# Gathering the narrow-tile products of sparse attention in TensorE's instruction order

## The chip, the cores and the metric

One core of a Trainium2 chip runs the whole program. The metric is the device time of one execution in microseconds, the median of several runs; lower is better.

## The reference, cut to what matters

One inference step of a decoder layer with two mixers that share one input projection, for a prompt of 256 tokens and 8 sample sequences of 8 tokens with 2,048 cached tokens each (320 token columns in all):

```python
u = rmsnorm(x) @ w_in                       # 2048 x 23664, split among all mixers
o_a = gated_delta(conv(qkv_a), z_a, ...)    # 32 heads of 128, recurrent state
o_cmp, idx = cmp_select(q, pos, kc, vc, ...)          # pooled blocks of keys; top-16 blocks per query
o_sel = select_sample(q, pos, idx, cache_k_sel, cache_v_sel, page_table, ...)
o_win = window_sample(q, pos, cache_k_win, cache_v_win, ...)
o_b = (g[0] * o_cmp + g[1] * o_sel + g[2] * o_win) * silu(z_b)
y = x + (sigmoid(m_a) * (o_a @ w_branch_a) + sigmoid(m_b) * (o_b @ w_branch_b)) @ w_out
```

For the sample sequences the sparse attention (o_cmp, o_sel, o_win) has few query rows: 4 heads of a group x 8 tokens are 32 rows, for each of 4 key groups. Everything is float32.

## The kernel before, in words

The dense projections are one long stream, `p_mm` (with `p_load`, `p_hi`, `p_lo`): weights come in tiles `wraw` of 1 MB through a ring of three (`NRC`), ScalarE rounds each piece of four 128-row blocks to float32r (`whi`), VectorE forms the rest (`wlo`), and TensorE adds three products `acc` of 128x320 per 128 rows. Rings of four pieces (`NHI`) let the splitting run ahead of the products by 48 products. This stream has the lowest priority; it fills TensorE where nothing else is ready.

Beside it run generators for the other work. In the sparse attention stage these are `prompt` (the prompt's attention, full tiles), `compressed` (pooling of the cached pages, `pp`, then scores `sc`, sums `ip`, output `oc`), `window` (512 cached keys per sequence) and, from about a third of the program on, two workers `sample`, four sequences each, that read all pages of the selected cache. `scores` transposes a page (`nt`), copies it (`kT`, by VectorE and ScalarE in turn) and multiplies it with the queries (`ns`); `weighted` transposes the weights (`nt` from `xs`), copies them (`pT`) and multiplies them with the pages of values (`op`). The products `pp`, `sc`, `ns`, `op`, `oc` have 32 output rows each; four of them, one per key group or page, lie side by side in column tiles of TensorE (128x32, or 64x32 for the 64 new keys). `mp` uses 32 rows (32x128). All other products and transpositions use the whole 128x128 array. Pages come through SyncE's queue into slots (`Feed`), 10 per worker (`SW`).

The order of all engines' instructions is fixed when the program is built. A class `Clock` holds an estimated time per engine and the estimated end of every tile's last write and read; a class `Run` holds the generators. Each generator yields what its next step needs: an engine's name with tiles, such as `("pe", e.sum)`, or a condition. `Run._start` (L354) turns this into the earliest start by the estimate: the engine's own time or the moment at which the inputs are ready, whichever is later. `Run.go` takes the step with the earliest start, the smaller rank where two are equal, and lets it emit its instructions. `Clock.narrow` says whether the last product used a part of the array; `Timed` adds 170 ns to the estimate where this changes (the line `if self.clock.narrow != part`).

Then comes the gated DeltaNet stage (`g_init`, `conv_stream`, `g2_stream`, `g3_stream` and more; its first TensorE products go to `bank`, its constants are `c`, `pk_gdn` and `pk_gini`), and at the end the projections of the two branches and `w_out`. After the sample stage `obS` is stored to `d_ob` through SyncE's queue, which holds its instructions in order.

Of the kernel before, what the change touches and what calls it, by code (L numbers as in the profile page):

```python
# [37 lines left out]
NRC = 3  # L38
NHI = 4
NPL = 4  # L40
CR = -1
OR = -4
NWP = 4
# [20 lines left out]
class Pack:  # L64
    def __init__(self, rows=P):
        self.at, self.parts, self.n, self.rows = {}, [], 0, rows
# [267 lines left out]
class Run:  # L334
# [2 lines left out]

    def __init__(self, clock):  # L340
        self.c, self.s = clock, []

    def add(self, gen, rank=0, at=None):
        x = [gen, None, (self.c.t["pe"], "sp") if at is None else at, rank]
# [12 lines left out]
    def _start(self, x):  # L357
        if callable(x[1]):
            while callable(x[1]):
                if not x[1]():  # L360
                    return None
                self._step(x)
                if x not in self.s:
                    return None
        y = x[1]
        e = y[0] if isinstance(y, tuple) else y
        if e == "exp":
            if self.c.lock:
                return None
            e = "act"  # L370
        if not isinstance(y, tuple):
            return max(self.c.t[e], self.c.after(x[2], e))
        return max([self.c.t[e]] + [self.c.after(a, e) if isinstance(a, tuple) else a.free(e) if isinstance(a, Next) else
                                    self.c.ready(e, a) for a in y[1:]])

    def go(self, until=lambda: False):
        while self.s and not until():
# [58 lines left out]
def step(ctx: ExitStack, tc: tile.TileContext, I, O):  # L436
    nc = tc.nc
    ctx.enter_context(tc.manual_schedule())
    clock = Clock()
# [39 lines left out]
    run = Run(clock)  # L479
# [688 lines left out]
    def pooled(b, kv):  # L1168
        pp = cps.tile([P, 512], F32, tag="a", name="pp")
        for i in range(0, 4, 2):  # L1170
            pg = []
            for _ in range(8):
                pg.append((yield from cfeed.get()))
            yield ("pe", *pg)
            for k in range(8):
                j = k % 4
                T.matmul(pp[32 * j:32 * j + 32], Pk[:, kv, i + k // 4], pg[k], start=i + k // 4 == 0, stop=i + k // 4 == 3)
            if i == 0:
                for j in range(3):
                    T.matmul(pp[32 * j:32 * j + 32], Pk[:, kv, 4], pg[j + 1], start=False, stop=False)  # L1180
            cfeed.release(8)
        yield "dve"
        pl = cp.tile([P, 512], F32, tag="c0", name="pl", bufs=1)
        V.tensor_tensor(pl.rearrange("p (g d) -> p g d", g=4), pp.rearrange("p (g d) -> p g d", g=4),
                        bc(cb[:, kv], [[0, 4], [1, P]]), op=OP.add)
        yield ("pe", clock.last, Next(cps, "a"))
        tp = cps.tile([P, 512], F32, tag="a", name="tp")
        for g in range(4):
            T.transpose(tp[:, g * P:g * P + P], pl[:, g * P:g * P + P], ident)
        yield "act"  # L1190
        pt = cp.tile([P, 512], F32, tag="c1", name="pt", bufs=1)
        S.activation(pt, tp, AF.Copy)
        yield "pe"
        return pt

    def compressed():
        for b in range(B):
            pt = yield from pooled(b, 0)
            yield lambda: done["q"] == 16
            yield ("pe", clock.last, Next(cps, "a"))  # L1200
            kp = cps.tile([P, 512], F32, tag="a", name="kp")
            T.matmul(kp, proj[:, 0], pt, start=True, stop=True)
            rs = yield from rstd(cp, cps, "a", kp, 512, (0, 512), ("c0", "c2", "c3"))
            kc = cp.tile([P, 512], F32, tag="c0", name="kc", bufs=1)
            V.scalar_tensor_tensor(kc, kp, gains[:, 1:2], rs, op0=OP.mult, op1=OP.mult)
            yield ("pe", clock.last, Next(cps, "a"))
            sc = cps.tile([P, 512], F32, tag="a", name="sc")
            for g in range(4):
                T.matmul(sc[32 * g:32 * g + 32, :127], qT(b, g), kc[:, g * P:g * P + 127], start=True, stop=True)
            yield "dve"  # L1210
            s1 = cp.tile([P, 127], F32, tag="s1", name="s1")
            V.scalar_tensor_tensor(s1, sc[:, :127], SCALE, cmpB[:, :127], op0=OP.mult, op1=OP.add)
            mx = cp.tile([P, 3], F32, tag="mxc", name="mxc")
            V.tensor_reduce(mx[:, 0:1], s1, axis=AX.X, op=OP.max)
            V.tensor_scalar(mx[:, 0:1], mx[:, 0:1], -1.0, None, op0=OP.mult)
            yield "act"
            S.activation(s1, s1, AF.Exp, bias=mx[:, 0:1], accum_out=mx[:, 1:2])
            yield "dve"
            V.reciprocal(mx[:, 2:3], mx[:, 1:2])
            V.tensor_scalar(s1, s1, mx[:, 2:3], None, op0=OP.mult)  # L1220
            yield ("pe", clock.last, Next(cps, "a"))
            ip = cps.tile([P, 512], F32, tag="a", name="ip")
            q = 32 * (b % 4)
            T.matmul(ip[q:q + 32, :127], N["G"], s1, start=True, stop=True)
            T.transpose(ip[:127, P:2 * P], s1, ident)
            yield "dve"
            V.tensor_copy(imp[q:q + 32, b // 4, :127], ip[q:q + 32, :127])
            sT = cp.tile([P, P], F32, tag="sT", name="sT")
            V.tensor_copy(sT[:127], ip[:127, P:2 * P])
            if b % 4 == 3:  # L1230
                yield from select(b // 4)
                done["sel"] = b // 4 + 1
            pt = yield from pooled(b, 1)
            vp = cps.tile([P, 512], F32, tag="a", name="vp")
            for g in range(4):
                T.matmul(vp[:, g * P:g * P + P], pt[:, g * P:g * P + P], proj[:, 1], start=True, stop=True)
            yield "dve"
            vc = cp.tile([P, 512], F32, tag="c0", name="vc", bufs=1)
            V.tensor_copy(vc, vp)
            yield ("pe", clock.last, Next(cps, "a"))  # L1240
            oc = cps.tile([P, 512], F32, tag="a", name="oc")
            for g in range(4):
                T.matmul(oc[32 * g:32 * g + 32, :P], sT[:127, 32 * g:32 * g + 32], vc[:127, g * P:g * P + P], start=True, stop=True)
            yield "dve"
            add_o(oc, gS[:, 0, b:b + 1], b)
            done["cmp"] = b + 1
# [55 lines left out]

    def new_scores(e, bs, kS, dst):

        yield ("pe", e.sum)
        ns = e.s("ns")
        for i, b in enumerate(bs):
            for g in range(4):
                T.matmul(ns[32 * g:32 * g + 32, 64 * i:64 * i + 64], qT(b, g), kS[:, g], start=True, stop=True)
        for i, b in enumerate(bs):  # L1310
            yield ("dve", ns)
            V.scalar_tensor_tensor(dst[:, i], ns[:, 64 * i:64 * i + 64], SCALE, newB[:, 56 - 8 * b:120 - 8 * b], op0=OP.mult, op1=OP.add)

    def scores(e, b, npg, finish):

        for quad in range(0, npg, 4):
            ks, ns = [], None
            for p in range(4):
                pg = yield from e.feed.get()
                yield ("pe", pg, e.next)  # L1320
                nt = e.t("nt")
                for g in range(4):
                    T.transpose(nt[:, g * P:g * P + P], pg[:, g * P:g * P + P], ident)
                e.feed.release()
                ks.append(e.x("kT", e.nk))
                if p % 2:
                    yield ("dve", nt)
                    V.tensor_copy(ks[-1], nt)
                else:
                    yield ("act", nt)  # L1330
                    S.activation(ks[-1], nt, AF.Copy)
                if len(ks) < e.nk:
                    continue
                yield ("pe", *ks, *([] if ns else [e.sum]))
                ns = ns or e.s("ns")
                for k, kT in enumerate(ks, p + 1 - e.nk):
                    for g in range(4):
                        T.matmul(ns[32 * g:32 * g + 32, k * P:k * P + P], qT(b, g), kT[:, g * P:g * P + P], start=True, stop=True)
                ks = []
            yield ("dve", ns)  # L1340
            finish(quad, ns)

    def weighted(e, b, npg, x, vS, op):

        pend = []
        for quad in [npg] + list(range(0, npg, 4)) + [None]:
# [8 lines left out]
            if quad not in (0, npg):  # L1355
# [2 lines left out]
                    for k in range(n0):  # L1358
                        got.append(((yield from e.feed.get()) if q0 < npg else vS, pT, k, m0))
                last = quad is None  # L1360
                yield ("pe", *[y[0] for y in got], *[y[3] for y in pend])
                for i, (pg, pT, k, m0) in enumerate(got):
                    for g in range(4):
                        T.matmul(op[32 * g:32 * g + 32], pT[:m0, k * P + 32 * g:k * P + 32 * g + 32], pg[:m0, g * P:g * P + P],
# [56 lines left out]
    def sample(smp, sps, n, bs):  # L1421
# [4 lines left out]
        for i, b in enumerate(bs):  # L1426
            yield lambda: done["sel"] > b // 4
            q = 32 * (b % 4)
            yield ("pe", selm, Next(sps, "s"))
            mp = sps.tile([P, 512], F32, tag="s", name="mp")  # L1430
            T.matmul(mp[:, :32], N["E"][q:q + 32], selm[q:q + 32, b // 4], start=True, stop=True)
            yield "dve"
# [782 lines left out]
        slab(I["w_branch_b"], DM, ((256 * f, 256),), KT, Later("b", 0), Later("b", 1), lambda f: True, take_b(2 * f), None, lambda k: fin["ob"] > k)  # L2215

    pj["gdn"] = True
    run.add(g_init())
    run.add(load_z_stream(), -1)
    run.add(conv_stream(), 2)  # L2220
# [126 lines left out]
```

## Time and profile before

| what | value |
|---|---|
| median of 3 runs | 2573.67 us (2572.28 to 2574.88) |
| the profiled execution | 2573.57 us, span 2571.4 us |
| TensorE busy | 2518.8 us, 98%, 22,220 records |
| TensorE's weight load | 2325.0 us, 90% |
| VectorE, ScalarE, GpSimd busy | 64%, 54%, 16% |
| granted TensorE clock, mean | 0.994 |
| DMA, mean | 214 GB/s, 549.12 MB |

TensorE is the engine to look at; a share of 98% says that it waits little, not that all its time is spent well. A record's length is its latency: products overlap, so costs are read from the distance of starts. All products are recorded under one line, L330, that of the helper that emits them, so groups are told apart by their tiles.

### The profile page before, as it was taken

What the parts mean: (1) busy time and instruction counts of PE and PEld (TensorE: products, weight loads), DVE (VectorE), ACT (ScalarE), POOL (GpSimd) and SP (SyncE); (2) the same over time, 40 slices, a digit from 0 to 9 for tenths busy, and PEclk for the clock granted to TensorE, in tenths of its full rate; (3) what the DMA queues carried; (4) which work ended last, traced back from release to release, by engine and by line L of the source; (5) the groups of instructions that cost most, each with busy time, mean ns of one, the idle gap of its engine ahead of it and who ended that gap; (6) DMA issues with size and microseconds to landing.
All of it is one profiled execution on the core that took longest, in us unless ns stands there. A gap on an engine that the chain in (4) does not pass through costs nothing.

```text
span 2571.4 us, 59460 instructions
## 1 busy us (share of the span) xinstructions
PE 2518.8 (98%) x22220; PEld 2325.0 (90%) x22220; DVE 1645.7 (64%) x4090; ACT 1400.4 (54%) x3290; POOL 413.2 (16%) x991
## 2 busy tenths in 40 slices
PE   7999999999999999999999999999999989999999
PEld 5898788888899888889999999998999979999999
DVE  5554455555756555544788788788797875555443
ACT  5453443444444333335777868777787755544443
POOL 2000001000000000000133234243334232000000
PEclk9999999999999999999999999999999999999999
DMA  6757777888875889985554655555456546765564
GB/s 197 236 165 250 240 250 280 280 295 303 277 254 180 317 273 316 320 260 171 169 177 138 194 161 172 162 171 176 135 173 192 193 147 211 229 195 180 185 194 126
DMA packets 553795, 549.12 MB, mean 214 GB/s; under 512 B 32994, under 2 KB 457107, under 8 KB 553123
## 3 DMA queue, kind: packets, MB, share of 16 engines
q1 hardware_dynamic: 538660, 496.30, 60.4%
q0 software_dynamic: 14848, 49.04, 5.3%
q8 instruction: 175, 2.87, 0.4%
q14 instruction: 112, 0.92, 0.1%
HBM read 472.93 MB, written 72.29 MB: 212 GB/s over the span
## 4 chain that ended last, share of the span: by engine, by line
PE 83%; issue 6%; DVE 5%; DMA 2%; POOL 2%; ACT 1%; SPq 0%; DVEq 0%; POOLq 0%; ACTq 0%
PE acc L330 60%; PE ps L330 6%; PE nt L330 3%; PE pp L330 3%; PE op L330 2%; PE ns L330 1%; POOL vx L330 1%; PE bank L330 1%; PE tp L330 1%; DVE wlo L330 1%; PE p L330 1%; PE ms L330 1%; PE pu L330 1%; PE sp L330 1%; DMA spg<-cache_k_sel 1%
## 5 line engine op out<-in xcount | busy, mean ns | idle before, releaser
L330 PE MATMUL acc<-hhi,whi 128*128 128x320 f32 (+1 forms) x3472 | 1154.8, 333 | 0.7 <-ACT hhi L330 0.7
L330 ACT ACTIVATE whi<-wraw 128x512 fp32r<-128x512 f32 (+1 forms) x996 | 625.8, 630 | 847.4 <-PE acc L330 797.5
L330 PE MATMUL acc<-hhi,wlo 128*128 128x320 f32 (+1 forms) x3472 | 1077.6, 310 | 0.7 <-DVE wlo L330 0.7
L330 PE MATMUL acc<-hlo,whi 128*128 128x320 f32 (+1 forms) x3472 | 1076.4, 310 | 0.1
L330 DVE TENSOR_TENSOR wlo<-wraw,whi 128x512 fp32r<-128x512 f32 x992 | 681.7, 691 | 529.3 <-ACT whi L330 501.0
L330 PEld LDWEIGHTS acc<-hhi,whi 128*128 128x128 f32 (+1 forms) x3472 | 657.8, 189 | 38.4 <-issue 29.6
L330 PEld LDWEIGHTS acc<-hlo,whi 128*128 128x128 f32 (+1 forms) x3472 | 658.2, 190 | 6.9 <-issue 2.6
L330 PEld LDWEIGHTS acc<-hhi,wlo 128*128 128x128 f32 (+1 forms) x3472 | 655.4, 189 | 0.9 <-DVE wlo L330 0.9
L330 PE MATMUL acc<-oah,whi 128*128 128x320 f32 x512 | 158.2, 309 | 0.0
L330 PE MATMUL acc<-oal,whi 128*128 128x320 f32 x512 | 158.2, 309 | 0.0
L330 PE MATMUL acc<-oah,wlo 128*128 128x320 f32 x512 | 158.2, 309 | 0.0
L330 POOL CAST vx<-v 32x128 fp32r<-32x128 f32 x256 | 97.8, 382 | 115.2 <-DVE v L330 84.2
L330 DVE SCALAR_TENSOR_TENSOR cv<-xp,cw,cv 128x344 f32<-128x344 f32 x192 | 111.0, 578 | 5.6 <-ACT cv L330 4.0
L298 POOL DMA_DIRECT2D d_mz<-raw x48 | 26.2, 545 | 466.8 <-ACT raw L330 418.8
L330 PEld LDWEIGHTS acc<-oah,whi 128*128 128x128 f32 x512 | 96.1, 188 | 0.0
L330 PEld LDWEIGHTS acc<-oal,whi 128*128 128x128 f32 x512 | 96.1, 188 | 0.0
L330 PEld LDWEIGHTS acc<-oah,wlo 128*128 128x128 f32 x512 | 96.1, 188 | 0.0
L330 DVE SCALAR_TENSOR_TENSOR sS<-sS,ends,pu 128x128 f32<-128x128 f32 x256 | 83.2, 339 | 14.5 <-PE pu L330 14.0
L330 DVE COPY kT<-nt 128x512 f32<-128x512 f32 x80 | 55.0, 690 | 57.7 <-PE nt L330 56.5
L330 PE MATMUL pp<-cpg,Pk 128*32 128x512 f32 x608 | 78.6, 598 | 0.0
L330 ACT ACTIVATE kT<-nt 128x512 f32<-128x512 f32 x80 | 47.1, 594 | 57.3 <-PE nt L330 57.2
L330 PE MATMUL nt<-pk_const,spg 128*128 128x128 f32 x512 | 76.1, 276 | 1.6 <-DMA spg<-cache_k_sel 1.6
(422 smaller groups left out, 3412.9 us busy)
## 6 DMA issues: line engine op xcount, KB each, us to landing
wraw<-w_in SPq DMA_DIRECT2D x120, 1024.0 KB
wraw<-w_in SPq DMA_DIRECT2D x129, 512.0 KB
cpg<-cache_k_cmp SPq DMA_DIRECT2D x128, 256.0 KB
cpg<-cache_v_cmp SPq DMA_DIRECT2D x128, 256.0 KB
spg<-cache_k_sel SPq DMA_DIRECT2D x128, 256.0 KB
spg<-cache_v_sel SPq DMA_DIRECT2D x128, 256.0 KB
wraw<-w_branch_a SPq DMA_DIRECT2D x32, 1024.0 KB
sS<-state_gdn SPq DMA_DIRECT2D x32, 512.0 KB
```

The source lines that it names most:

```text
L298: return f(*a, **k)
L330: return f(*a, **k)
```

## The change

A step whose products go to narrow tiles now yields `"tiles"` instead of `"pe"`. For the sparse attention (`run.gather` is true until the DeltaNet stage) `_start` changes its estimate: while the last product was a wide one, a `tiles` step counts as startable 3,000 ns (`HOLD`) after its inputs are ready; while the last one was narrow, every other TensorE step counts as startable 400 ns (`STICK`) after the engine is free. Nothing else differs; no tile, buffer or product is added or taken away.

```diff
+HOLD, STICK = 3000, 400
...
-        self.c, self.s = clock, []
+        self.c, self.s, self.gather = clock, [], True
...
+        tiles = e == "tiles"
+        if tiles:
+            e = "pe"
         if not isinstance(y, tuple):
-            return max(self.c.t[e], self.c.after(x[2], e))
-        return max([self.c.t[e]] + [self.c.after(a, e) if isinstance(a, tuple) else a.free(e) if isinstance(a, Next) else
-                                    self.c.ready(e, a) for a in y[1:]])
+            r = self.c.after(x[2], e)
+        else:
+            r = max([0.0] + [self.c.after(a, e) if isinstance(a, tuple) else a.free(e) if isinstance(a, Next) else
+                             self.c.ready(e, a) for a in y[1:]])
+        if e == "pe" and self.gather and tiles != self.c.narrow:
+            if tiles:
+                return max(self.c.t[e], r + HOLD)
+            return max(self.c.t[e] + STICK, r)
+        return max(self.c.t[e], r)
...
-            yield ("pe", *pg)
+            yield ("tiles", *pg)
...
+    run.gather = False
```

The same word stands in the steps of `pp`, `sc`, `oc`, `ns` (three places), `op` and `mp`; `ip` stays a `"pe"` step.

What the planner made of it, at three places (`acc` are the projection products, `spg` pages of the selected cache, a name's number of products in a row stands behind it).

TensorE, the sample stage, two workers reading keys; before:

```order
L330 MATMUL ns<-kT,qs 32x128 x16
L330 MATMUL nt<-pk_const,spg 128x128 x8
L330 MATMUL acc<-hhi,whi 128x320
L330 MATMUL acc<-hlo,whi 128x320
L330 MATMUL acc<-hhi,wlo 128x320
L330 MATMUL nt<-pk_const,spg 128x128 x4
L330 MATMUL ns<-kT,qs 32x128 x16
L330 MATMUL acc<-hhi,whi 128x320
L330 MATMUL acc<-hlo,whi 128x320
L330 MATMUL acc<-hhi,wlo 128x320
L330 MATMUL nt<-pk_const,spg 128x128 x8
```

The change:

```order
L331 MATMUL ns<-kT,qs 32x128 x16
L331 MATMUL nt<-pk_const,spg 128x128 x28
L331 MATMUL acc<-hhi,whi 128x320
L331 MATMUL acc<-hlo,whi 128x320
L331 MATMUL acc<-hhi,wlo 128x320
...
L331 MATMUL ns<-kT,qs 32x128 x32
L331 MATMUL nt<-pk_const,spg 128x128 x32
L331 MATMUL acc<-hhi,whi 128x320
L331 MATMUL acc<-hlo,whi 128x320
L331 MATMUL acc<-hhi,wlo 128x320
```

The `ns` of one worker, 16 products, stood alone between transpositions and projection products; now those of both workers stand together, 32 products, with 27 projection products (nine times the three rows) ahead of them and 28 to 32 transpositions in a row behind.

TensorE, the start of the sample stage: the scores against the new keys (`ns` from `ksS`) and the masks `mp` of the first sequences; before:

```order
L330 MATMUL ns<-ksS,qs 32x64 x32
L330 MATMUL acc<-hhi,whi 128x320
L330 MATMUL acc<-hlo,whi 128x320
L330 MATMUL acc<-hhi,wlo 128x320
...
L330 MATMUL acc<-hhi,whi 128x320
L330 MATMUL acc<-hlo,whi 128x320
L330 MATMUL acc<-hhi,wlo 128x320
L330 MATMUL mp<-selm,pk_nsa 128x32
L330 MATMUL acc<-hhi,whi 128x320
```

The change:

```order
L331 MATMUL ns<-ksS,qs 32x64 x32
L331 MATMUL acc<-hhi,whi 128x320
L331 MATMUL acc<-hlo,whi 128x320
L331 MATMUL acc<-hhi,wlo 128x320
...
L331 MATMUL acc<-hhi,whi 128x320
L331 MATMUL acc<-hlo,whi 128x320
L331 MATMUL acc<-hhi,wlo 128x320
L331 MATMUL mp<-selm,pk_nsa 128x32 x2
L331 MATMUL nt<-pk_const,spg 128x128 x4
```

Between `ns` and the first `mp` stood 9 projection products, and now 30; the two `mp` now stand together, and the first transposition of a page directly behind them.

SyncE, the turn to the DeltaNet stage: the last weight tiles of the stage, the store of `obS`, the weight tiles and constants of the next stage; before:

```order
L298 DMA wraw<-w_in 128x8x128 x4
L298 DMA d_ob<-obS 128x16x64
L298 DMA wraw<-w_in 128x8x128 x2
L298 DMA c_16040<-gdn_conv_w 64x4x128
L298 DMA al<-gdn_a_log 128x32
L298 DMA al<-gdn_dt_bias 128x32
L298 DMA gn<-gdn_norm_g 128x1
L298 DMA pk_gdn<-c_gdn 128x600
L298 DMA pk_gini<-c_gini 128x640
```

The change:

```order
L299 DMA d_ob<-obS 128x16x64
L299 DMA wraw<-w_in 128x8x128 x4
L299 DMA wraw<-w_in 128x8x256
L299 DMA c_16118<-gdn_conv_w 64x4x128
L299 DMA al<-gdn_a_log 128x32
L299 DMA al<-gdn_dt_bias 128x32
L299 DMA gn<-gdn_norm_g 128x1
L299 DMA pk_gdn<-c_gdn 128x600
L299 DMA pk_gini<-c_gini 128x640
```

A tile of 1 MB is one transfer of 128x8x256 or two of 128x8x128. Between the store and the constant `c` stood one tile, and now three; the number of projection products between the last `tp` of the sample stage and the first `bank` product is 111 in both.

## Rows read from the trace of the kernel before

**Rows 1.** The page of the profile, its parts 1 and 2: TensorE's busy time, its share and number of records; TensorE's busy share and granted clock in 40 slices of the span (tenths, 9 is 90% or more).

```profile
PE 2518.8 (98%) x22220; PEld 2325.0 (90%) x22220; DVE 1645.7 (64%) x4090; ACT 1400.4 (54%) x3290; POOL 413.2 (16%) x991
...
PE   7999999999999999999999999999999989999999
...
PEclk9999999999999999999999999999999999999999
```

**Rows 2.** The table of stretches (us from the start of the span): length, busy time and records of TensorE, its weight load, VectorE, ScalarE and GpSimd, granted clock, mean busy share of the DMA engines, GB/s.

```profile
64.00:843.00 779.00, 775.68 (x5985) 671.00 (x5983) 440.40 (x1073) 339.54 (x737) 48.52 (x90) 1.00 0.74 249
843.00:1152.00 309.00, 305.27 (x3798) 277.54 (x3798) 167.50 (x283) 121.20 (x209) 13.03 (x28) 0.99 0.91 303
...
1165.00:2160.00 995.00, 973.65 (x9382) 924.40 (x9382) 791.99 (x2308) 721.29 (x1957) 326.58 (x841) 0.99 0.55 169
```

**Rows 3.** TensorE's list of waits: which product waited for whom; us in total, times, the longest.

```profile
PE bank L330 <- DMA pk_gini<-c_gini: 4.1, 1, 4.1
...
PE mp L330 <- DVE xn L330: 2.5, 1, 2.5
...
PE nt L330 <- DMA spg<-cache_k_sel: 1.6, 4, 0.5
...
PE bank L330 <- DMA c<-gdn_conv_w: 1.2, 1, 1.2
```

**Rows 4.** The chain that ended last, one piece of it late in the program: start, us, what.

```profile
2464.59 7.04 PE acc L330 x48
```

**Rows 5.** Timeline of TensorE in the sample stage, around one `ns` that stands alone between projection products: start, us of the group, engine, operation, out<-in, rows*columns of the tile, shapes, number of records (a float32 product has two, a transposition or a float32r product one).

```profile
852.96 0.31 PE L330 MATMUL acc<-hhi,wlo 128*128 128x320 f32 x1
853.20 1.08 PE L330 MATMUL ns<-kT,qs 128*32 128x128 f32 x32
854.21 0.41 PE L330 MATMUL acc<-hhi,whi 128*128 128x320 f32 x1
854.47 0.30 PE L330 MATMUL acc<-hlo,whi 128*128 128x320 f32 x1
...
854.75 0.60 PE L330 MATMUL nt<-pk_const,spg 128*128 128x128 f32 x4
855.11 0.39 PE L330 MATMUL acc<-hhi,whi 128*128 128x320 f32 x1
```

**Rows 6.** The same view, where an `ns` is followed by another narrow product.

```profile
923.92 1.08 PE L330 MATMUL ns<-kT,qs 128*32 128x128 f32 x32
924.82 1.06 PE L330 MATMUL op<-spg,pT 128*32 128x128 f32 x32
925.80 0.66 PE L330 MATMUL nt<-pk_const,spg 128*128 128x128 f32 x4
926.22 0.39 PE L330 MATMUL acc<-hhi,whi 128*128 128x320 f32 x1
```

**Rows 7.** The same view, two narrow shapes behind each other (64 rows and 128 rows, 32 columns each).

```profile
1019.55 0.42 PE L330 MATMUL op<-vsS,pTn 64*32 64x128 f32 x8
1019.90 1.08 PE L330 MATMUL op<-spg,pT 128*32 128x128 f32 x32
```

**Rows 8.** Timeline of all engines at the start of the sample stage (in brackets the idle time before, and who ended it; SPq is the queue of SyncE).

```profile
842.17 1.14 DVE L330 SCALAR_TENSOR_TENSOR xn<-ns,newB 128x64 f32<-128x64 f32 x8 [3.46 <-DMA d_ob<-ob]
842.23 0.90 SPq L298 DMA_DIRECT2D spg<-cache_k_sel  x2
...
842.94 0.38 PE L330 MATMUL mp<-selm,pk_nsa 32*128 32x32 f32 x2 [2.55 <-DVE xn L330]
...
847.37 1.05 PE L330 MATMUL nt<-pk_const,spg 128*128 128x128 f32 x4
```

**Rows 9.** Two short stretches of the table (columns as in rows 2), and TensorE's timeline in the first of them and at a wait of its own for a page.

```profile
843.40:850.20 6.80, 6.80 (x27) 6.32 (x28) 2.18 (x7) 1.23 (x2) 0.00 (x0) 0.50 0.93 308
1154.00:1160.80 6.80, 3.85 (x14) 3.73 (x15) 1.39 (x4) 0.75 (x2) 0.00 (x0) 0.50 1.11 333
...
846.04 0.47 PE L330 MATMUL acc<-hlo,whi 128*128 128x320 f32 x1
846.30 0.47 PE L330 MATMUL acc<-hhi,wlo 128*128 128x320 f32 x1
...
965.11 0.43 PE L330 MATMUL op<-spg,pT 128*32 128x128 f32 x8 [0.96 <-DMA spg<-cache_v_sel]
```

**Rows 10.** Timeline of TensorE and of SyncE's queue at the turn to the DeltaNet stage.

```profile
1134.72 0.27 PE L330 MATMUL tp<-pk_const,o 128*128 128x128 f32 x1
...
1146.39 1.00 SPq L298 DMA_DIRECT2D wraw<-w_in  x2
...
1150.69 0.46 SPq L298 DMA_DIRECT2D pk_gini<-c_gini  x1
...
1156.95 0.69 PE L330 MATMUL bank<-bag,pk_gini 64*128 64x64 f32 x2 [4.06 <-DMA pk_gini<-c_gini]
```

**Rows 11.** DMA issues of the whole program (operation, times, KB each), and VectorE's reading of `ns` in the sample stage from the groups of instructions (times, busy us, mean ns, idle before).

```profile
wraw<-w_in SPq DMA_DIRECT2D x120, 1024.0 KB
...
spg<-cache_k_sel SPq DMA_DIRECT2D x128, 256.0 KB
...
L330 DVE SCALAR_TENSOR_TENSOR xs<-ns,m 128x512 f32<-128x512 f32 x30 | 20.7, 690 | 20.7 <-PE ns L330 20.6
```

More of the change, by code (lines that the diff above doesn't have):

```diff
@@ L1205, in compressed @@
             V.scalar_tensor_tensor(kc, kp, gains[:, 1:2], rs, op0=OP.mult, op1=OP.mult)
-            yield ("pe", clock.last, Next(cps, "a"))
+            yield ("tiles", clock.last, Next(cps, "a"))
             sc = cps.tile([P, 512], F32, tag="a", name="sc")
@@ L1239, in compressed @@
             V.tensor_copy(vc, vp)
-            yield ("pe", clock.last, Next(cps, "a"))
+            yield ("tiles", clock.last, Next(cps, "a"))
             oc = cps.tile([P, 512], F32, tag="a", name="oc")
@@ L1303, in new_scores @@
     def new_scores(e, bs, kS, dst):
-        yield ("pe", e.sum)
+        yield ("tiles", e.sum)
         ns = e.s("ns")
@@ L1333, in scores @@
                     continue
-                yield ("pe", *ks, *([] if ns else [e.sum]))
+                yield ("tiles", *ks, *([] if ns else [e.sum]))
                 ns = ns or e.s("ns")
@@ L1360, in weighted @@
                 last = quad is None
-                yield ("pe", *[y[0] for y in got], *[y[3] for y in pend])
+                yield ("tiles", *[y[0] for y in got], *[y[3] for y in pend])
                 for i, (pg, pT, k, m0) in enumerate(got):
@@ L1428, in sample @@
             q = 32 * (b % 4)
-            yield ("pe", selm, Next(sps, "s"))
+            yield ("tiles", selm, Next(sps, "s"))
             mp = sps.tile([P, 512], F32, tag="s", name="mp")
```

## The prediction

> **What bounds the kernel now.** I read the busy shares first: TensorE is busy for 98% of the span, and apart from the first slice every slice shows it at 8 tenths or more, at full granted clock [rows 1]. So only two things can move the time: what TensorE's own sequence costs, and the few holes in it. The table by stage says where the holes lie [rows 2]. In the 779 us from 64 to 843 the engine misses 3.3 us, in the sample stage (843 to 1152) 3.7 us; the gated DeltaNet stage (1165 to 2160) misses 21 us. The list of TensorE's waits names the single ones in reach of this change: 4.1 and 1.2 us at the first product of the DeltaNet stage, 2.5 us at `mp`, 1.6 us for pages of the selected cache [rows 3].
>
> A busy engine can still do nothing useful, so I read the order of instructions next, and then the timeline of TensorE at a few changes of tile shape. The order shows what no view of the profile does: up to the first `bank` product the tile shape changes 425 times in the kernel before. What a change costs is read from starts, since matmuls overlap. In a plain stretch 48 projection products take 7.04 us, 0.147 us each [rows 4].
>
> - **Into narrow tiles:** the last projection product before a lone `ns` starts at 852.96 and `ns` at 853.20: 0.24 instead of 0.147, so **0.09 us** [rows 5].
> - **Out, to a projection product:** the lone `ns` holds the engine for 1.01 us (853.20 to 854.21), the same 32 records followed by another narrow step only 0.90 (923.92 to 924.82); the first projection product after it takes 0.26 instead of 0.147. Together 0.11 + 0.11 = **0.22 us** [rows 5, 6].
> - **Out, to a transposition:** `op` takes 0.98 (0.08 over 0.90), the four transpositions behind it 0.42 where four after a projection product take 0.36: **0.14 us** [rows 5, 6].
> - **Between two narrow shapes:** the 8 records of `op` with 64 rows (two groups of four) take 0.35 before the 128-row ones; eight such groups take 0.90, two would take 0.22: **0.13 us** [rows 6, 7].
>
> **The change part by part.** It adds and removes no instruction on TensorE, VectorE, ScalarE or GpSimd. It moves them: the planner puts a narrow step 3 us later than it could start, unless TensorE is in narrow tiles already, and puts everything else 0.4 us later while it is. From the first transposition of `hist` on, the order of all engines is the one of before, apart from a few weight loads; so the last 9,757 matmuls of the program, the stage with 21 us of holes among them, should cost what they did. On SP four reads of the page table fall away (56 to 52). There are four terms.
>
> *Changes of tile shape.* Counted in the two orders up to the first `bank` product (narrow means 32 rows or 32 columns): entries 158 to 121, exits to a projection product 90 to 40, exits to transpositions and other wide products 69 to 82, changes between narrow shapes 19 to 27; 89 among wide shapes stay. 425 changes become 359. The sum is -37 x 0.09 - 50 x 0.22 + 13 x 0.14 + 8 x 0.13 = -3.3 - 11.0 + 1.8 + 1.0 = **-11.5 us**. All of it lies on TensorE's own sequence in stretches with 99% busy time [rows 2], so nothing hides it. If the 13 exits cost 0.22 as well it is -10.5; with half the error the other way -12.
>
> *The start of the sample stage.* Before, 9 projection products stand between `ns` and `mp`, and TensorE waits 2.55 us: VectorE's `xn` could not start before 842.17, when the store of `d_ob` had landed [rows 8]. Behind the wait the granted clock fell to one half (1.2 GHz) from 843.4 to 850.2, where a projection product takes 0.26 to 0.27 instead of 0.147; 6.8 us x 0.45 = 3.1 us lost [rows 9]. Now 30 products stand there, 21 more, 21 x 0.147 = 3.1 us: the wait for `xn` is covered. What is late next are the pages: SP issues the first at 842.23 [rows 8], for the same landing, and TensorE now wants it at about 843.9 (`mp` reached at 840.4 + 3.1, two `mp` products, no others between). The trace of before shows only that the page was there at 847.37. The new wait lies between 0 and 3.2 us; I take 2, the middle and a bit, as 256 KB also have to be moved. Without a fall of the clock that leaves -5.6 + 2 = **-3.5 us**; ends -5.6 (no wait) and 0 (a wait of 2.5 us that again turns the clock down).
> The Trainium skill ("TensorE: Matmul & The Clock Gate", part 1 on the HAM clock gate) says that the clock falls when the engine has idled and comes back with activity. The trace agrees: a fall behind 2.55 us [rows 9], none behind 0.96 us at 965.11 [rows 9]. By that rule the end 0 is as good as the end -5.6 for a wait between the two.
>
> *The turn to the DeltaNet stage.* Here SP's queue decides. Before, one weight tile stands between the store of `obS` and the DeltaNet constants; it goes out at 1146.39, 11.7 us after the last `tp`, since it waits until an older tile is split, and `pk_gini` goes out at 1150.69 and is waited for until 1156.95 [rows 10]. Now three tiles stand there, and TensorE reaches `bank` after the same 111 projection products. The third waits for the split of the last tile of the stage, which by the four pieces of lead comes some 45 products, 6.6 us, and a split later, at about 8 us: 3 us earlier than before. Against that stand 2 MB more in front; at 303 GB/s [rows 2] a tile of 1,024 KB [rows 11] is 3.5 us, but the first tiles go while the third still waits. I take **-2 us**; ends -7.0 (both waits gone, and with them 45% of the 3.85 us that it worked at half clock behind them [rows 9]) and +6.6 (all of the 2 MB adds).
>
> *Waits that are new.* I looked in the order for products that need a copy by VectorE or ScalarE of what TensorE wrote less than 0.66 us of work before. There was one between 150 and 1010 us of TensorE's work; now there are eight, such as `sp` directly behind the `op` whose bank it needs, in prompt(). A step of VectorE between two products costs up to 0.77 us (`xn` at 842.17, `mp` at 842.94 [rows 8]): between 0 and 6.2 us. Most of the eight have some work between, so I take **+2 us**.
>
> Sum: -11.5 - 3.5 - 2 + 2 = **-15.0**. The profiled execution took 2573.57 us (its span is 2571.4; 2.2 us lie around it), which is 0.1 us under the median of the three runs; 2573.57 - 15.0 = **2558.6 us**.
>
> **The rivals.**
>
> 1. *The gathered steps pile up their results.* Two workers' `ns` now end together, and VectorE must read both (`xs`, 0.69 us each [rows 11]) before either PSUM bank is free. If TensorE waits for one such reading in each of 16 pairs, 11.0 us come back: 2569.7, no change. Against it: 32 transpositions (8 x 0.42 [rows 6]) and 27 projection products (27 x 0.147), 7.4 us, stand between two such pairs in the new order. The Trainium skill ("TensorEngine Tiling (Array Packing)", section PSUM Bottleneck) warns that after tiling the PSUM copy may be the bound; no row of before shows TensorE waiting for `xs`.
> 2. *Slower: page loads fall behind the bunches.* A round in the new order (32 `ns`, 32 transpositions, 27 projection products) takes 1.9 (1.01 + 0.87) + 3.4 + 4.0 = 9.3 us and eats 8 pages of 256 KB and 9 x 64 KB of weights [rows 11], 2.7 MB; that needs 289 GB/s. The sample stage moved 303 GB/s with 0.91 of the DMA time, the stage before it 249 [rows 2]. At 303 a round fits; at 249 it misses 1.5 us, 24 us over 16 rounds: 2583. Slower than before from 0.94 us a round, at 264 GB/s. For it: TensorE waited for `spg` already [rows 3]. Against: the stage holds 240 more projection products for the same pages, and 20 page slots are filled ahead.
> 3. *More than forecast:* no new wait and the turn without a wait: -11.5 - 5.6 - 7.0 = -24.1, 2549.5.
> 4. *The turn gets worse:* all of the 2 MB counts: -11.5 - 3.5 + 6.6 + 2 = -6.4, 2567.2.
> 5. That the order doesn't do what it says is excluded: 425 changes against 359.
>
> **How the numbers follow.** A measurement of this kernel can tell about 0.2%, 5.1 us, from no change. Forecast 0.60, rival 1 0.14, rival 2 0.06, rival 3 0.12, rival 4 0.08. The forecast with its neighbours 3 and 4 gives faster 0.80; rival 1 gives 0.14 for no change; rival 2 gives slower 0.06. The range reaches up over rival 4 to rival 1 and down to rival 3: 2549 to 2571.
>
> **What would show it.** TensorE's waits without `mp <- xn`, the clock at full after 840, and `ns` in runs of 64 records with about 1.9 us each confirm terms one and two. Term one alone is seen from a stretch without waits: the same set of products from 64 us to the first page product in less busy time. The wait at `bank` tells term three. Many waits of `nt` or `op` for `spg` above 10 us in all would be rival 2, waits for `xs` rival 1. The forecast is wrong if the stage from 1165 on, whose order did not change, changes its length by more than 3 us, or if busy time before it does not fall by about 11 us.

## The result and the profile after

The changed kernel takes **2552.03 us** (median of 4 runs, 2548.57 to 2554.88), the one before 2572.98 us beside it: ratio 0.9921, 95% interval 0.9906 to 0.9936. It is 21 us faster in the medians and 18.7 in the profiled executions (2554.88 against 2573.57; spans 2553.1 and 2571.4). The forecast was 15 us.

The page after, against [rows 1]: busy time falls by 15.6 us, its share stays at 98%; one slice now has a lower clock.

```profile
PE 2503.2 (98%) x22220; PEld 2326.4 (91%) x22220; DVE 1642.9 (64%) x4090; ACT 1400.0 (55%) x3290; POOL 415.2 (16%) x991
...
PE   7999999999999999999999999999999989999999
...
PEclk9999999999999999999999999999999989999999
```

To compare like with like, I cut both spans at the same work: at the 91st projection product and at the first `bank` product. Table of stretches of before, then of after (columns as in [rows 2]):

```profile
53.80:1152.46 1098.66, 1091.15 (x9850) 958.61 (x9849) 613.43 (x1366) 466.49 (x957) 61.55 (x117) 1.00 0.79 265
1152.46:2571.40 1418.94, 1388.81 (x12211) 1338.61 (x12211) 1001.55 (x2666) 905.60 (x2286) 335.54 (x857) 0.99 0.57 175
```

```profile
54.50:1154.11 1099.61, 1094.54 (x9995) 979.32 (x9993) 618.31 (x1378) 474.49 (x972) 63.86 (x122) 1.00 0.80 268
1154.11:2553.10 1398.99, 1370.87 (x12067) 1320.09 (x12067) 993.85 (x2655) 897.18 (x2271) 335.19 (x852) 0.99 0.57 175
```

The first stretch is 0.95 us longer, but 144 more projection products lie in it (the order has 4,770 in place of 4,626 before `bank`), 21.1 us at 0.147 each [rows 4]. So this work became **20.2 us** shorter. The second stretch is 19.95 us shorter, but the products that left it are worth 21.1: like for like it is 1.2 us longer.

TensorE's waits after, against [rows 3]: `mp` is off the list, so are `nt` and `op` with `spg`, and `bank <- pk_gini` is 1.0 us shorter. New are the first page of the sample stage (the list names `d_mz`, a store; what the product reads is the page `spg`) and four short ones.

```profile
PE bank L331 <- DMA pk_gini<-c_gini: 3.1, 1, 3.1
...
PE nt L331 <- DMA d_mz<-raw: 2.1, 1, 2.1
...
PE tp L331 <- DVE s L331: 0.8, 1, 0.8
PE sp L331 <- DVE ob L331: 0.8, 1, 0.8
...
PE op L331 <- ACT pT L331: 0.6, 2, 0.5
```

The start of the sample stage after (timeline; against [rows 8]). VectorE's `xn` starts at 819.10, SP sends the first page at 819.08, TensorE runs its projection products up to `mp` without a hole, then waits for the page; projection products behind it are 0.27 us apart.

```profile
819.08 5.15 SPq L299 DMA_DIRECT2D spg<-cache_k_sel  x9
...
819.10 0.23 DVE L331 SCALAR_TENSOR_TENSOR xn<-ns,newB 128x64 f32<-128x64 f32 x1 [4.61 <-DMA d_ob<-ob]
...
820.54 0.48 PE L331 MATMUL mp<-selm,pk_nsa 32*128 32x32 f32 x4
823.13 1.09 PE L331 MATMUL nt<-pk_const,spg 128*128 128x128 f32 x4 [2.11 <-DMA d_mz<-raw]
...
824.28 0.47 PE L331 MATMUL acc<-hlo,whi 128*128 128x320 f32 x1
824.55 0.47 PE L331 MATMUL acc<-hhi,wlo 128*128 128x320 f32 x1
```

The half clock there and at the turn (stretches of after, against [rows 9]):

```profile
822.80:826.20 3.40, 3.07 (x13) 3.06 (x14) 0.57 (x2) 0.60 (x1) 0.00 (x0) 0.50 0.97 321
1157.30:1164.10 6.80, 6.48 (x24) 6.37 (x25) 1.94 (x6) 1.65 (x5) 0.00 (x0) 0.50 0.61 170
```

The turn to the DeltaNet stage after (against [rows 10]):

```profile
1151.22 0.43 SPq L299 DMA_DIRECT2D pk_gini<-c_gini  x1
...
1157.62 0.68 PE L331 MATMUL bank<-bag,pk_gini 64*128 64x64 f32 x2 [3.08 <-DMA pk_gini<-c_gini]
```

**What none of these views shows.** In pooling, four `pp` products run side by side, each in its own 32 columns of the engine. Where their pages land one by one, a quad breaks apart. TensorE's timeline of before, and its weight load's, at one such place:

```profile
86.72 4.65 PE L330 MATMUL pp<-cpg,Pk 128*32 128x512 f32 x22
...
87.28 0.14 PEld L330 LDWEIGHTS pp<-cpg,Pk 128*32 128x32 f32 x2 [0.41 <-DMA cpg<-cache_k_cmp]
88.03 0.14 PEld L330 LDWEIGHTS pp<-cpg,Pk 128*32 128x32 f32 x2 [0.61 <-DMA cpg<-cache_k_cmp]
88.68 0.14 PEld L330 LDWEIGHTS pp<-cpg,Pk 128*32 128x32 f32 x2 [0.51 <-DMA cpg<-cache_k_cmp]
...
91.30 0.42 PE L330 MATMUL acc<-hhi,whi 128*128 128x320 f32 x1
```

The same 22 records in after, 3.8 us later, when the pages are there:

```profile
90.54 2.78 PE L331 MATMUL pp<-cpg,Pk 128*32 128x512 f32 x22
93.24 0.81 PE L331 MATMUL ms<-sq,pk_const 128*128 128x320 f32 x2
```

From start to the next product 4.58 us became 2.70. A `pp` record is 0.59 us long and the weight loads that wait for the pages start 0.65 to 0.75 us apart, so the records cover the holes: the engine counts as busy, and the list of TensorE's waits has no entry. Only the weight load's waits, seen by tile, show it in before:

```profile
  DMA cpg<-cache_k_cmp: 2.7, 5
  DMA cpg<-cache_v_cmp: 1.6, 3
```

Three bunches are stretched so in before: 1.87 us over the 2.71 of others here, 0.89 over 1.85 at 326, 0.65 at 406. Together **3.4 us**; none in after. The same holds for all runs below: no bunch is stretched by a page where `pp` is held, and one to three are in every kernel where it isn't (before and runs 3, 4, 5, 6, 9).

### The profile page after: what moved, and what is told of

Same layout as the page of the kernel before. It is cut to its first block, busy times and chain, and to the rows that moved or that the text cites. A ratio compares the mean times of both kernels' runs of the same rounds, so it can differ in the third digit from the quotient of the medians.

```text
span 2553.1 us, 59455 instructions
## 1 busy us (share of the span) xinstructions
PE 2503.2 (98%) x22220; PEld 2326.4 (91%) x22220; DVE 1642.9 (64%) x4090; ACT 1400.0 (55%) x3290; POOL 415.2 (16%) x991
## 4 chain that ended last, share of the span: by engine, by line
PE 73%; issue 17%; DVE 4%; POOL 3%; DMA 1%; ACT 1%; SPq 1%; POOLq 0%; DVEq 0%; ACTq 0%
PE acc L331 55%; PE ps L331 6%; PE nt L331 3%; PE op L331 1%; PE pp L331 1%; POOL vx L331 1%; PE ns L331 1%; PE bank L331 1%; PE p L331 1%; PE pu L331 1%; POOL d_mz L299 1%; DVE wlo L331 1%; PE tp L331 1%; PE ms L331 1%; SPq L299 1%
## 5 line engine op out<-in xcount | busy, mean ns | idle before, releaser
L331 DVE SCALAR_TENSOR_TENSOR sS<-sS,ends,pu 128x128 f32<-128x128 f32 x256 | 83.0, 339 | 14.3 <-PE pu L331 13.9
```

The source lines that it names most:

```text
L331: return f(*a, **k)
```

## The experiments

All were timed beside the kernel before. The first expectations carry three theories: A (the changes of tile shape, some 10 us, and the 3 us by which narrow steps now come behind the landing of their pages, some 7 us in pooling and 2 to 3 in listed waits), B (changes of shape alone, at a higher price), C (the lead alone).

For each profiled execution I took the change of the span against before apart as above. *Idle* is recorded idle time of TensorE before `bank`; *clock* 45% of the time at half clock before `bank` [rows 9]; *quads* the stretched pooling bunches; *rest* is what is left of the stretch up to `bank`, per equal work. *Prices* is the forecast's sum of its four prices over the order's changes of shape. *Start* is what lies ahead of the 91st projection product. All in us, from one execution each. The differences named in the text go by the ratio; medians and these single executions can differ from them by up to 5 us (run 1: -10.5 by the ratio, -14.6 in the medians, -15.7 here). Runs 5 and 6 keep the order of before up to `bank` and so show how much a row can tell: taken apart in the same way, their rest is -0.2 and -0.6, their start -1.2 and -2.4.

| kernel | changes | prices | rest | idle | clock | quads | start | from `bank` | sum |
|---|---|---|---|---|---|---|---|---|---|
| before | 425 | 0 | 0 (idle 7.5) | 0 | 0 (6.8 at half) | 0 (3.4) | 0 | 0 | 0 |
| the change | 359 | -11.5 | -12.9 | -2.4 | -1.5 | -3.4 | +0.7 | +1.2 | -18.3 |
| the change again | 359 | -11.5 | -12.7 | -1.0 | -1.5 | -3.4 | -0.1 | +0.6 | -18.2 |
| held always | 416 | -2.2 | -4.3 | -3.0 | -3.1 | -3.4 | -2.4 | +0.5 | -15.7 |
| pooling held alone | 427 | -0.5 | +0.6 | -2.4 | -1.5 | -3.4 | -1.8 | -4.0 | -12.5 |
| pooling not held | 369 | -10.2 | -13.0 | +12.8 | +6.2 | -2.5 | +0.7 | 0.0 | +4.2 |
| stick without hold | 419 | -2.4 | -2.2 | -2.7 | 0.0 | -0.8 | +0.1 | -5.1 | -10.7 |
| hold 6, stick 0.8 | 323 | -16.9 | -20.7 | +28.6 | +15.4 | -3.4 | -1.5 | +0.6 | +19.0 |
| not held, more filler | 369 | -10.1 | -11.7 | -4.3 | 0.0 | -2.3 | -2.0 | +11.9 | -8.4 |
| hold 6, more filler | 326 | -16.3 | -21.0 | +12.9 | +6.2 | -3.4 | -2.6 | +33.3 | +25.4 |
| hold 3, stick 1.5 | 335 | -15.9 | -12.6 | +21.9 | +1.5 | -3.4 | -2.6 | +5.9 | +10.7 |
| hold without stick | 377 | -8.5 | -11.5 | +2.1 | 0.0 | -3.4 | -2.4 | +1.3 | -13.9 |

**1. The lead without the gathering.** Every narrow step is held 3 us, also among narrow ones; nothing sticks.

```diff
-        if e == "pe" and self.gather and tiles != self.c.narrow:
-            if tiles:
-                return max(self.c.t[e], r + HOLD)
-            return max(self.c.t[e] + STICK, r)
+        if tiles and self.gather:
+            return max(self.c.t[e], r + HOLD)
```

> A narrow step counts as startable 3 us after its inputs in every case, also while TensorE is in narrow tiles already, and nothing sticks: the lead without the gathering. The order has 416 changes of tile shape up to the first bank product (before 425, changed kernel 359); by the four prices of the prediction that is worth -2.2 us. Theory A (two causes: fewer shape changes, about 10 us, and a lead of 3 us over pages that land later than the planner reckons, about 7 us in pp and 2 to 3 elsewhere): faster by 9 to 12 us, about 2562. Theory B (shape changes alone, each worth more than read from the starts, 21 us / 66 = 0.32 us): 9 fewer, -3 us, about 2570. Theory C (the lead alone): about -20, 2553.

2557.6 us, ratio 0.9959 (0.9946 to 0.9973), about -10.5: as A had it, while B (-3) and C (-20) missed. Half of the gain comes with nine changes of shape less. But the table says that A's 7 us in pooling were wrong: 3.4 are quads, the others are waits (3.0) and half clock (3.1).

**2. Pooling alone is held**, the other narrow steps go back to `"pe"` (all else as in 1).

> Only the pooling products pp are held 3 us, always; all other steps are as before and nothing sticks. 427 changes of shape. Theory A: the quads of pp that fell apart because pages landed one by one (12 extra groups of 0.43 us and some shorter gaps, about 7 us in the trace of before) come whole: -6 to -8 us, about 2566. Theory B: no change, 2573.

2559.83 us, 0.9956 (0.9942 to 0.9969), -11.4, more than A's 6 to 8. The quads give 3.4 of it, all that they had cost. One bunch is still long, 4.36 us from start to the next product, but no page is waited for there: the granted clock is at half (timeline, then the stretch).

```profile
749.70 4.43 PE L331 MATMUL pp<-cpg,Pk 128*32 128x512 f32 x22
...
749.70:753.00 3.30, 3.30 (x17) 0.79 (x19) 2.76 (x7) 0.00 (x0) 0.00 (x0) 0.50 0.62 161
```

4.0 lie from `bank` on, which no theory had: the wait for `pk_gini` is gone there.

**3. Everything but pooling is gathered** (`"tiles0"` counts as narrow, but is not held).

```diff
-            yield ("tiles", *pg)
+            yield ("tiles0", *pg)
...
-                return max(self.c.t[e], r + HOLD)
+                return max(self.c.t[e], r if now else r + HOLD)
```

> The changed kernel, but the pp step counts as startable as soon as its pages are there, also while TensorE is in wide tiles; the other narrow steps are held and the rest sticks as in the change. 369 changes of shape, worth -10.2 us by the four prices. Theory A: the lead over the pages of pp is gone, so -12 to -14 us, about 2560, and single pp records in the trace again. Theory B: 56 changes at 0.32, -18 us, about 2555.

2575.05 us, 1.0009 (0.9998 to 1.002): no gain, and A and B both missed. The rest, put down to the changes of shape, is -13.0 us, and 12.8 us of idle time and 6.2 of half clock took them back. TensorE's waits in this kernel:

```profile
PE acc L331 <- ACT whi L331: 6.9, 1, 6.9
...
PE nt L331 <- ACT xs L331: 4.5, 1, 4.5
```

**4. Sticking without holding** (`HOLD, STICK = 0, 400`).

> HOLD 0, STICK 400: nothing is held, only the other steps wait a little behind a narrow one. 419 changes of shape, worth -2.4 us by the four prices (25 fewer exits to a projection product, 22 more to other wide products). Theory A: -2 to -4 us, about 2570. Theory B: -2 us, 2571. Theory C: none, 2573.

2558.92 us, 0.9953 (0.994 to 0.9967), -12 where at most 4 were expected by all. Shapes give 2.2 of it; 5.1 come from `bank` on, as in 2: `pk_gini` is waited for 0.46 us.

**5 and 6. The price by itself.** 128 added products of 32 columns, one in every block of the branch-a projections, in a narrow tile (5) or a whole one (6).

```diff
+                    if q["kt"] == 32 and k % 4 == 2:
+                        T.matmul(dm_[0][:32, :32], ident[:, :32], ident[:, :32], start=True, stop=True)
# 6: dm_[0][:P, :32], ident[:, :P]
```

> The kernel before with 128 added products of 32 columns, one before every fourth group of three projection products of the branch-a stage, into a PSUM bank that nobody reads; the stationary part has 32 columns, so each one is an entry into a narrow tile and an exit to a projection product. To be read against the same with a wide tile (e6). Prices of the prediction: 128 x (0.09 + 0.22) = 40 us more than e6. If each change were worth 0.32 us (theory B): 128 x 0.64 = 82 us more than e6.

> The kernel before with the same 128 added products, the stationary part with all 128 columns: no change of tile shape. Both theories: 128 products of two passes with 32 moving columns, 0.06 to 0.11 us each, 7 to 14 us over the kernel before, and nothing else.

Narrow 2619.46 us, 1.0186 (1.0173 to 1.0199); wide 2600.39, 1.0115 (1.01 to 1.013). The difference is 19 us, less than either theory gave (40 and 82): the whole-tile product, expected at 7 to 14 us over before, took 29 and is no free control. Timeline of the narrow one, then TensorE and its weight load in the wide one:

```profile
2301.23 0.31 PE L330 MATMUL acc<-oah,wlo 128*128 128x320 f32 x1
2301.47 0.25 PE L330 MATMUL dmt<-pk_const 128*32 128x32 f32 x2
2301.65 0.42 PE L330 MATMUL acc<-oah,whi 128*128 128x320 f32 x1
2301.91 0.31 PE L330 MATMUL acc<-oal,whi 128*128 128x320 f32 x1
```

```profile
2300.83 0.30 PE L330 MATMUL dmt<-pk_const 128*128 128x32 f32 x2
2300.97 0.39 PE L330 MATMUL acc<-oah,whi 128*128 128x320 f32 x1
2301.20 0.31 PE L330 MATMUL acc<-oal,whi 128*128 128x320 f32 x1
...
2300.69 0.33 PEld L330 LDWEIGHTS dmt<-pk_const 128*128 128x128 f32 x2
```

Way in: 0.24 in place of 0.147, 0.09 more, the forecast's figure again in another stage. The first projection product behind takes 0.26, 0.11 more, as in the forecast; but behind the whole-tile product it takes 0.23 (2300.97 to 2301.20), 0.08 more, without a change of shape, so this part alone is no price. From `acc` to `acc` over the narrow one 0.68 us pass where two plain steps take 0.29: 0.39 x 128 = 50 us, where the medians differ by 48. So a pair of changes, with the product between, costs 0.39, which excludes B's 0.64 for the pair alone. How much of the 0.18 between `dmt` and `acc` is the product's own stays open.

**7. Fewer changes still** (`HOLD, STICK = 6000, 800`).

> The changed kernel with HOLD 6000 and STICK 800. 323 changes of shape, worth -16.9 us by the four prices against before, 5.4 us more than the changed kernel's -11.5. Theory A: the page lead is as good or better, new short waits cost 0 to 4 us: 2545 to 2551, faster than the changed kernel by 1 to 6 us. Theory B: 36 fewer changes at 0.32, 11 us below the changed kernel, 2541.

2592.51 us, 1.0082 (1.0067 to 1.0096): the fewest changes of all, a rest of -20.7, and 21 us slower in the medians. Timeline of TensorE at the end of its sample stage:

```profile
1160.42 0.33 PE L331 MATMUL tp<-pk_const,o 128*128 128x128 f32 x1
1166.59 2.13 PE L331 MATMUL nt<-pk_const,xs 128*64 128x128 f32 x9 [5.84 <-ACT xs L331]
...
1177.90 0.48 PE L331 MATMUL tp<-pk_const,o 128*128 128x128 f32 x1 [0.47 <-DVE o L331]
1185.17 0.63 PE L331 MATMUL acc<-hhi,whi 128*128 128x320 f32 x1 [6.80 <-ACT whi L331]
```

VectorE and ScalarE in the first of these waits:

```profile
1160.56 0.69 DVE L331 SCALAR_TENSOR_TENSOR xs<-ns,m 128x512 f32<-128x512 f32 x1 [0.52 <-PE ns L331]
...
1161.75 2.35 DVE L331 TENSOR_REDUCE mx<-xs 128x1 f32<-128x2112 f32 x1
...
1164.39 2.06 ACT L331 ACTIVATE xs<-xs,mx 128x2112 f32<-128x2112 f32 x1 [5.56 <-DVE mx L331]
```

The transposition waits for a whole softmax: its last scores are read out of PSUM in 0.69 us, then come the maximum (2.35) and the exponential (2.06). No projection product lies between these waits. That gave theory R: a projection product is the filler that hides the softmax chains, at most 4,776 of them came before `bank` in these orders, and each delay of narrow steps pulls filler forward. The orders agree: behind the last sample page 117 are left in before and in the change, but 24 here and in experiment 3.

**8. The change again.**

> The changed kernel itself, on the chip of e5 to e7, to compare e7 with. All theories: 2549 to 2555.

2552.46 us, 0.9926 (0.9913 to 0.9938), as expected.

**9 and 10. More filler for 3 and 7**: three more gate slabs ahead of the DeltaNet stage, in 10 also two slabs of z. 11 is the change with `STICK = 1500`, which leaves 105 products behind the last page.

```diff
-NM = 3
+NM = 0
# 10 also: ZS = (..., 28, 30, 31, 29, 27)
```

> The kernel in which all but the pooling products are gathered (2575.05 us), with three more slabs of the last mixer gate handed out before the DeltaNet stage, so 198 more projection products stand before its first product `bank` (4,974 in place of 4,776) and no stretch of the sample stage is without them: 114 of them are left behind the last sample page, where the kernel of 2575.05 us had 24. Theory R (that kernel lost its gain because the projection products ran out before the sample stage ended, and TensorE then waited for the softmax, then for new weights, at half clock): its idle time before `bank` falls from 20.3 to about 8 us and the half clock from 20.5 to about 9, so 2558 us (2553 to 2563), still behind the change because pooling's quads break. Theory S (gathering without the lead makes TensorE wait by itself): 2570 to 2580, idle time before `bank` near 20. Theory T (the products are missed in the DeltaNet stage, from where they were taken): idle time before `bank` falls, but `bank` to the end grows by over 6 us: 2564 to 2572.

> The kernel with 6 us of hold and 0.8 us of sticking (2592.51 us, 323 changes of tile shape before the DeltaNet stage), with 480 more projection products handed out before that stage (three slabs of the last mixer gate, two of z): 5,256 in place of 4,776. 326 changes. Theory R (projection products ran out there): the 36 us of idle time and 41 us of half clock before `bank` fall to about 8 and 9: 2592.5 - 28 - 14 = 2550 us (2543 to 2558). Theory S (a long hold makes TensorE wait by itself, for the softmax chains that it holds up): 2580 to 2595. Theory T (the products are missed in the DeltaNet stage): idle time before `bank` falls, `bank` to the end grows by 6 to 20 us: 2556 to 2570.

> The change with 1.5 us of sticking in place of 0.4: 335 changes of tile shape before the DeltaNet stage in place of 359, worth 4.4 us more by the four prices, and 105 projection products left behind the last sample page, so they don't run out. Theory R with the four prices: 2548 us (2544 to 2552), some 4 below the change. Theory S (more sticking delays the narrow steps that the softmax chains wait for): 2553 to 2565, with more idle time than the change's 5 us before `bank`. The lead alone (changes of shape worth nothing): 2552, as the change.

Run 9: 2563.55 us, 0.9953 (0.994 to 0.9966). The idle time before `bank` fell from 20.3 to 3.2 us and the half clock from 20.5 to 6.8: R's cause is shown for experiment 3. From `bank` on it became 11.9 us longer, as T said: the 198 products were missed there. The time lies between R's range (to 2563) and T's (from 2564). Its waits, the first of them 3.9 in the change:

```profile
PE bank L331 <- DVE kqP L331: 9.7, 2, 6.0
...
PE acc L331 <- ACT hhi L331: 3.8, 2, 2.2
PE acc L331 <- ACT whi L331: 3.3, 1, 3.3
```

Run 10: 2602.2 us, 1.011 (1.0097 to 1.0123), slower than 7, against R and T, and above S's 2580 to 2595 too. The 12.6 us for `xs` are gone, but the idle time fell only from 36.1 to 20.4, since TensorE now waited 7.3 us for `whi` at the turn (5,232 of its 5,256 products were gone by the last sample page), and what follows `bank` paid 33 us for 480 products.

Run 11: 2583.18 us, 1.0031 (1.002 to 1.0042). R (2548) failed; S was right that the run is slower than the change, but had neither the size (2553 to 2565) nor the cause. Here the filler does not run out; the largest wait in all comes from sticking itself (timeline):

```profile
106.75 0.61 PE L331 MATMUL pp<-cpg,Pk 128*32 128x512 f32 x4
108.25 0.66 PE L331 MATMUL tp<-pk_const,pl 128*128 128x128 f32 x4 [0.89 <-DVE pl L331]
```

This wait comes 13 times (its list of waits):

```profile
PE tp L331 <- DVE pl L331: 10.7, 13, 1.0
```

With 1.5 us added to every wide step, the planner can no longer tell a `tp` that is ready in 0.9 us from a projection product that is ready now, and emits `tp` first; this follows from `_start`, and the 13 waits fit it. With 0.4 us there is no such wait. The other half of the 21.9 us is spread over many waits (2.4 for `osum`, 2.3 more than before for pages of the selected cache, 1.4 more at `mp`); what sticking has to do with them is not shown.

**12. Holding without sticking** (`HOLD, STICK = 3000, 0`).

> The change with its hold of 3 us and no sticking: 377 changes of tile shape before the DeltaNet stage, worth 8.5 us by the four prices (the change's 359: 11.5); 33 projection products left behind the last sample page, so they nearly run out only at the very end. Theory R with the four prices (shape by its prices, the lead over the pages as in the change, sticking's own short waits gone): 2573 - 8.5 - 7 - 2 - 2 = 2553.5 us (2550 to 2557), the change's time within what can be told: idle time before `bank` 3 to 5 us. Theory S (sticking as such delays work, 0.4 us as 1.5 us did, only less): 2546 to 2550, faster than the change. The lead alone: 2553 too, so this run speaks to sticking and not to that.

2560.61 us, 0.9959 (0.9945 to 0.9973), 7 us over R's 2553.5. The short waits of sticking are gone and the rest is -11.5, but at the turn TensorE waited for a weight tile, with half the clock behind it; 33 products were left behind the last page.

```profile
PE acc L331 <- ACT whi L331: 7.1, 1, 7.1
```

No variant beat the change. One thing is left: in 2 and 4 the part from `bank` on is 4 to 5 us shorter. The change's order with that turn was not run.

## Why the prediction was right, and where it was not

**Direction and range** held, and so did the largest term. That the sum of -15.0 came near the -18.3 of the spans is in part luck: two terms were too large, and a gain of 7.1 us that the forecast did not have made up for them. Term by term:

1. *Changes of shape*, forecast -11.5: measured -12.9 and, again, -12.7, as a remainder. Over eleven profiled runs the remainder follows the four prices (-0.5 to -16.9 forecast, +0.6 to -21.0 found) and is 1.2 to 4.7 us larger in eight; runs 2, 4 and 11 are smaller (+0.6 for -0.5, -2.2 for -2.4, -12.6 for -15.9). The term stands, mis-sized by 1.4 us. Of its figures the way in was found again in run 5, which bounds both ways together by 0.39. A rival that the prediction lacks: up to `bank` the switches between projection products and other whole-tile products also fell, from 603 to 563 by the traces. They cost nothing. From start to start, four transpositions take 0.36 us (854.75 to 855.11 [rows 5]) and the first projection product behind them 0.23 (to 855.34), together 0.59; and 4 x 0.111 + 0.147 is 0.59 too, with the 0.111 us that each of 32 transpositions in a row takes in the change (from 842.24 on).
2. *Start of the sample stage*, forecast -3.5: -2.55 for `mp`, +2.11 for the page (I had taken 2), and half the clock gain: 3.4 us at half clock remain, -1.5 in place of -3.1. Sum -2.0. The step that failed is "without a fall of the clock": a wait of 2.1 us was followed by one. The Trainium skill ("TensorE: Matmul & The Clock Gate", part 1) has the clock fall when the engine has idled. The trace agrees, here behind 2.1 us. (Two slips in the working: -5.6 + 2 is -3.6, and from 843.9 to 847.37 the wait could have been 3.5 us, not 3.2.)
3. *The turn*, forecast -2: `bank <- c` fell from 1.19 to 0.43, `pk_gini` by 1.0, but the half clock behind it is worked through for 6.48 us in place of 3.85, +1.2. Sum about -0.6. `pk_gini` goes out 14.1 us behind the last `tp` (1137.13) in place of 16.0 [rows 10], 1.9 us earlier where 3 were taken. The 2 MB of weights in front cost nothing: `pk_gini` lands 6.3 to 6.4 us behind its issue in before (1150.69 to 1156.95), in the change (1151.22 to 1157.62) and in run 4.
4. *New short waits*, forecast +2: 0.8 + 0.8 + 0.6 = 2.2.
5. *What was missed*: 3.4 us of quads, and 3.7 us of listed waits that went away: 1.6 (`nt`) and 1.4 (`op`) for sample pages, 0.7 for one `acc` behind `wlo`. The quads are the hold's other effect, which the forecast never priced: a step that starts 3 us later finds its pages landed. For the listed waits this is not shown: `nt` is not held, `op`'s waits are gone in run 4 too, without a hold, and in the change run again (8) a wait of 1.2 us for a page came back. I had read "3.3 us missed in 779" [rows 2] as the whole of what pages could cost there; the records of `pp` hid the rest.

The terms 1 to 4 make -13.3 and with the fifth -20.4. The 2.1 us to -18.3 are the start (+0.7), some 1.0 from `bank` on, and small waits; their cause is open.

The mark that I had named, 11 us less busy time before `bank`, gave 1091.15 - (1094.54 - 21.1) = 17.7 less: 12.9 + 3.4 + 1.5, since stretched quads and half clock count as busy. The other one held: the DeltaNet stage and what follows stayed within 1.2 us.

**Rivals.** Rival 1 (waits for `xs`) does not occur in the change. In run 7 TensorE does wait for `xs` (12.6 us in three waits), but by another mechanism than the rival's: for the softmax, of which reading `ns` out of PSUM is 0.69 us. The Trainium skill ("TensorEngine Tiling (Array Packing)", section PSUM Bottleneck) warns that after tiling the PSUM copy may be the bound. No run here shows that. Rival 2 (page loads) did not come: waits for `spg` went away, but for the first page, and 1.2 us in run 8. Rival 3's time (2549.5) is nearer to the median than the forecast's (2558.6), but not for its reason: a new wait of 2.1 us came, and 3.1 us of the wait for `pk_gini` stayed. Rival 4 fell with the turn.

What stays open: the 1 to 5 us by which the remainder differs from the prices in single runs. The start's -2.6 to +0.7 needs no cause in the variants: runs 5 and 6, with the order of before, have -1.2 and -2.4.

## What to carry to other kernels

Count the changes of tile shape in the instruction order and price each way from start to start; here about 0.3 us for going in and out, which held within 5 us over nine other orders. Then ask what else a delay does: it gives transfers time to land (a gain that long records hide, to be looked for in the weight load's waits), and it uses up the filler that hides other chains, here the 117 products left over at the end of the stage. The best setting was not the one with the fewest changes: 359 gave 21 us, 323 lost 21.

## What the runs showed of the hardware

A product of 32 columns in a whole tile is not cheap: with two weight loads of 128 columns (0.33 us) it adds 0.22 us to a stream of projection products (experiment 6), over half of the 0.39 of a narrow one. The granted clock fell to its lower level (1.2 GHz) behind a 2.1 us wait (822.8, for 3.4 us) as behind 2.55 [rows 9]. The length of a wait alone does not tell it: the clock also fell behind 1.27 us in run 11 (at 749.2) and behind 0.69, 0.33 and 0.47 us close together in run 2 (at 749.7), but not behind 1.86 us in run 4 (at 1046), nor in the first stretch of run 11, with eleven idle holes of 0.89 to 1.0 us up to 590. Products in different column tiles overlap fully only where their operands are there together: the same 22 records took 2.70 us, and 4.58 us where the weight loads had to wait for the pages, 0.65 to 0.75 us apart.
